# A hybrid decoder layer on one core: bonus sums from a split operand, inverse blocks moved by DMA, the pooling branch placed earlier, four staging buffers

## The chip, the cores and the metric

The kernel runs on one core of a Trainium2 chip. The metric is the time on the device in microseconds (us); lower is better. All data are fp32 in HBM. TensorE (PE) multiplies, VectorE (DVE) and ScalarE (ACT) do element work, GpSimd (POOL) does small memsets and copies, and nearly all DMAs are issued from SyncE's queue (SP).

## The reference, cut to what matters

One layer, 1024 tokens of width 1024: a projection `z = h @ w_in`, an RWKV-7 branch with 8 heads of 64, a pooling branch with windows of 2, 4, 8 and 16, an output projection with a layer norm, and then an FFN with another.

```
w_log = -softplus(-(w0 + tanh(wd) @ wl_up)) - 0.5
decay = exp(-exp(w_log))
...
# the scan over tokens, per head: state S of 64 x 64
Sa = S @ a;  S = S * w + Sa b^T + v k^T;  y = S @ r
...
var = mean(square(y - m))                    # over the 64 channels of a head
y = (y - m) * rsqrt(var + GN_EPS) * lnx_g + lnx_b
y = y + sum(r * k * r_k) * v                 # the bonus: a sum over the channels of a head
y = y * g
...
mix = concat(y_a, y_b) @ w_out;  h = LN(ALPHA * h + mix)
```

## The kernel before

The program is written in an order, and a scheduler places each instruction on its engine's queue by that order as a priority and by what is ready; the queues are then fixed. `solve` runs at high priority.

**Stages.** Input norm and projections (`z_shift`, products `pz`) come first. The scan is cut into eight tasks t = 4 s + p: s is a half of 512 tokens, p one of four groups of two heads. `fr(t)` (lines 690 to 697) makes or reloads r, k and v of a task and calls `front`. Two tasks make a pair, and `solve` (699) calls `gram`, `inverse` and `chain` for it; `chain` ends in `post`. The loop of line 707 runs `fr(t + 2)`, `fr(t + 3)` and then `solve` for pair t / 2. The pooling groups (`pool_group`, `pool_out`) stand behind that loop, at line 712; then come the weights of the output projection (`out_weights`, 727), the products `pm` of `mix` (737), and the FFN.

**front (362).** All its products with 128x512 results go through one PSUM buffer, the tag "pa" (`psa`, 194, bufs=1): pw, pq, pss, pbo and pv in turn. The decay is a polynomial of t1 = tanh(...): one ScalarE step (379), five VectorE steps (380, 381), one ScalarE step (385), and then two VectorE scans (387, 391). The bonus is `rb` (421), a product with the 0/1 matrix `bones` (423) in full fp32, which the chip runs as two passes, and a multiply by v (425). Its small tiles come from the tag "k2", six buffers.

**inverse (462).** The Gram blocks of a pair, gB, hold for each half q of the pair eight chunks of 64 x 64, and their 16 x 16 diagonal blocks are inverted by VectorE in the layout of one block per partition. To get there, `dg` (472) masks the diagonal blocks, `dc` (474) packs them by a reduction, and two DMAs (476, 477) take them through DRAM to `ab`; line 478 subtracts dg from gB. VectorE's steps of lines 488 to 512 make the inverse blocks in `ef`, once as they are and once transposed. Two DMAs per q (516, 518) bring them back as `cc`, and four multiplies with `bmask` (521) spread them over E_ and F_. Then come the products pn (535, with F_) and pzz (539, with E_).

**post (597).** ScalarE squares y, a product with `jm` (1/64 in each head's block) sums, ScalarE gives a first reciprocal root, three VectorE steps (607 to 609) refine it by one Newton step, and three more finish.

**Staging.** The weights of the output projection are loaded in 16 pieces into the tag "o" with two buffers (732, 754), and each is split by ScalarE (734) and VectorE (735) into two fp32r parts. The tiles `wo` take the place of the activations hT, which are free when the last pooling projection is done, and pool "a4" takes the place of the pooling branch's tiles (`zpool.close()`).

An fp32r operand runs in one pass; where fp32 precision is wanted, the kernel splits it in a high part (a ScalarE copy to fp32r) and a low part (a VectorE subtraction).

## Time and profile before

| what | value |
|---|---|
| median of 3 runs | 1354.23 us (1353.0 to 1354.93) |
| the profiled execution | 1357.52 us |
| its span | 1355.8 us |
| busy: PE, DVE, ACT | 1309.3, 1023.8, 526.9 us |

The span runs from the first to the last instruction of the profiled execution; the execution's own time is a little longer. A busy time is the union of an engine's instruction intervals. Matmuls overlap in a pipe, so the mean time of one is longer than their distance: what a matmul costs is read from a run of many. The idle time before an instruction is shown in brackets, with what ended it.

### The profile page before, as it was taken

Reading aid. Unit: us, or ns where it says so; the run is one execution under the profiler, and the core shown is the slowest. Engines: PE = TensorE matmul, PEld = TensorE weight load, DVE = VectorE, ACT = ScalarE, POOL = GpSimd, SP = SyncE. Lnnn points to the kernel's source line nnn. Section 1 sums busy time; section 2 is a strip of 40 time slices with the busy share of each in tenths; the row PEclk is TensorE's granted clock in tenths of the full one; section 3 lists DMA queues with packets and bytes.
Section 4 is the critical chain, followed back from the end, with each engine's and each line's share of the span. In section 5 each row is a group of like instructions: output and inputs, shape, how many; then the busy total and the mean of one; then the engine's idle time right before and its main releaser. Section 6 shows DMA issues by size and latency. Waiting matters only on the chain.

```text
span 1355.8 us, 22923 instructions
## 1 busy us (share of the span) xinstructions
PE 1309.3 (97%) x9028; PEld 1029.2 (76%) x9028; DVE 1023.8 (76%) x1807; ACT 526.9 (39%) x889; POOL 12.8 (1%) x48
## 2 busy tenths in 40 slices
PE   6999999999997989999999999999999999999997
PEld 5787777777666667778888888888888888887886
DVE  6937566569698884556889989777766767987868
ACT  5823432244334511176434333223333334553530
POOL 0000000000000000000000000000000000000000
PEclk9999999999998999999999999999999999999999
DMA  8621130122123343263433336332323237987803
GB/s 280 216 107 51 55 75 10 59 78 55 41 58 103 91 120 93 102 215 131 150 107 117 114 113 224 116 110 102 101 79 107 101 119 261 319 282 249 264 24 124
DMA packets 117101, 173.52 MB, mean 128 GB/s; under 512 B 34688, under 2 KB 43904, under 8 KB 116992
## 3 DMA queue, kind: packets, MB, share of 16 engines
q1 hardware_dynamic: 116848, 172.01, 38.8%
q8 instruction: 71, 1.16, 0.4%
q14 instruction: 38, 0.31, 0.1%
q10 hardware_dynamic: 144, 0.04, 0.0%
HBM read 124.03 MB, written 47.97 MB: 127 GB/s over the span
## 4 chain that ended last, share of the span: by engine, by line
PE 73%; DVE 14%; DMA 8%; ACT 3%; issue 2%; SPq 0%; DVEq 0%; ACTq 0%
PE p L49 31%; PE pz L49 10%; PE pgt L49 7%; PE py L49 6%; PE pm L49 5%; PE px L49 4%; DMA ar<-a_d 2%; PE pzz L49 1%; PE pg L49 1%; PE cw L49 1%; PE cs L49 1%; DMA ab<-d 1%; DMA wdr<-ff_down 1%; DVE da L830 1%; PE cu L49 1%
## 5 line engine op out<-in xcount | busy, mean ns | idle before, releaser
L49 PE MATMUL p<-tb,p 128*128 128x512 f32 x1056 | 253.0, 395 | 0.0
L49 PEld LDWEIGHTS p<-tb,p 128*128 128x128 f32 x1056 | 198.7, 188 | 47.0
L49 PE MATMUL pz<-hT,wh 128*128 128x512 f32 x576 | 190.9, 406 | 0.0
L49 PE MATMUL p<-h,p 128*128 128x512 f32 x792 | 188.6, 392 | 0.0
L49 PEld LDWEIGHTS p<-h,p 128*128 128x128 f32 x792 | 148.7, 188 | 33.0
L829 ACT CAST p<-a 128x512 fp32r<-128x512 f32 x132 | 81.2, 622 | 181.3 <-PE p L49 138.4
L49 PEld LDWEIGHTS pz<-hT,wh 128*128 128x128 f32 x576 | 107.4, 188 | 32.9 <-issue 4.7
L49 PE MATMUL pz<-hT,wl 128*128 128x512 f32 x288 | 117.5, 408 | 0.0
L830 DVE TENSOR_TENSOR p<-a,p 128x512 fp32r<-128x512 f32 x132 | 89.3, 687 | 12.5 <-ACT p L829 12.1
L49 PE MATMUL pm<-wo,mh 128*128 128x512 f32 x224 | 78.6, 418 | 3.3 <-DVE o L764 1.4
L1001 DVE TENSOR_TENSOR u<-p,u 128x512 f32<-128x512 f32 x66 | 45.3, 687 | 31.6 <-PE p L49 31.6
L49 PEld LDWEIGHTS pz<-hT,wl 128*128 128x128 f32 x288 | 54.1, 188 | 16.5 <-issue 3.8
L49 PE MATMUL px<-da 128*128 128x512 f32 x276 | 64.3, 390 | 0.0
L49 PEld LDWEIGHTS px<-da 128*128 128x128 f32 x276 | 51.8, 188 | 10.9
L49 PEld LDWEIGHTS pm<-wo,mh 128*128 128x128 f32 x224 | 41.3, 188 | 15.8 <-ACT wo L734 1.9
L245 DVE TENSOR_TENSOR wl<-wr,wh 128x512 fp32r<-128x512 f32 x36 | 24.7, 688 | 35.1 <-ACT wh L243 34.3
L49 PE MATMUL pgt<-wg,h 128*128 128x512 f32 x192 | 48.4, 396 | 0.0
L49 PE MATMUL py<-da 128*128 128x512 f32 x204 | 47.7, 389 | 0.0
L49 PE MATMUL pm<-wo,ml 128*128 128x512 f32 x112 | 46.6, 419 | 0.0
L49 PEld LDWEIGHTS py<-da 128*128 128x128 f32 x204 | 38.3, 188 | 8.1
L243 ACT CAST wh<-wr 128x512 fp32r<-128x512 f32 x36 | 22.3, 619 | 56.3 <-PE pz L49 31.8
L1022 DVE TENSOR_TENSOR gs<-p,u 128x512 f32<-128x512 f32 x44 | 30.4, 690 | 18.1 <-PE p L49 17.3
(325 smaller groups left out, 2351.0 us busy)
## 6 DMA issues: line engine op xcount, KB each, us to landing
ar<-a_d SPq DMA_DIRECT2D x77, 256.0 KB, 4.2
wdr<-ff_down SPq DMA_DIRECT2D x55, 256.0 KB, 3.8
a<-ff_gate SPq DMA_DIRECT2D x44, 256.0 KB, 2.8
a<-ff_up SPq DMA_DIRECT2D x44, 256.0 KB, 2.8
a_d<-s SPq DMA_DIRECT2D x44, 256.0 KB, 2.3
b<-ff_down SPq DMA_DIRECT2D x22, 512.0 KB, 5.8
wr<-w_in SPq DMA_DIRECT2D x36, 256.0 KB, 2.8
a_d<-gs SPq DMA_DIRECT2D x33, 256.0 KB, 2.2
```

The lines of the kernel that those rows point to most:

```text
L49: PE.matmul(o, lhsT=l, rhs=r, start=a, stop=z)
L243: S.copy(wh, wr)
L245: V.tensor_tensor(wl, wr, wh.bitcast(F32), ALU.subtract)
L829: S.copy(h, r)
L830: V.tensor_tensor(l, r, h.bitcast(F32), ALU.subtract)
L1001: V.tensor_tensor(t, ps, u, ALU.add)
L1022: V.tensor_tensor(d, ps, u, ALU.add)
```

## The change

- The bonus sums: rb is split into a high and a low fp32r part, and two products with an fp32r copy of the 0/1 matrix replace the one in fp32 (`heads`).
- The decay: the polynomial of degree six is written as a product of three squares plus constants; ScalarE makes the squares, VectorE takes two steps.
- The inverse: gB goes to DRAM as whole rows, in two DMAs per half pair (64 partitions each), into a layout in which a second view reads the diagonal blocks out. The inverse blocks are written into DRAM tiles (`d2`) that are zero elsewhere, filled once from ScalarE's queue, and read back as full E_ and F_. The masks and the packing on VectorE go; gB is multiplied by a mask of zeros on the diagonal blocks instead of the subtraction, behind the DMAs in the program.
- Post: the square is scaled ahead of the sum, so `bones` serves and `jm` goes; the Newton step takes one square on ScalarE and two steps on VectorE; a factor of -0.5 goes into the column `hlg`.
- The pooling groups stand ahead of `fr(6)` and `fr(7)` in the program's order.
- The tag "o" has four buffers.

The lists QB, QE and QS hold the constants of the three squares; that hunk is left out.

```diff
@@ -65,10 +67,10 @@
     V.memset(bones[64:128, 64:128], 1.0)
-    jm = cq.tile([128, 128], F32, name="jm")
-    V.tensor_scalar(jm, bones, 1.0 / 64, None, ALU.mult)
+    bonr = cq.tile([128, 128], F32R, name="bonr")
+    V.tensor_copy(bonr, bones)
     cmat = cq.tile([128, 128], F32, name="cmat")
-    V.tensor_tensor(cmat, ident, jm, ALU.subtract)
+    V.scalar_tensor_tensor(cmat, bones, -1.0 / 64, ident, ALU.mult, ALU.add)
     gmask = cq.tile([128, 128], F32, name="gmask")
@@ -83,6 +85,9 @@
                         compare_op=ALU.is_ge, fill=0.0, base=15, channel_multiplier=-1)
+    omask = cq.tile([128, 64], F32, name="omask")
+    V.tensor_scalar(omask.rearrange("p (q t) -> p q t", q=4), bmask[:, :, None].to_broadcast([128, 4, 16]),
+                    -1.0, 1.0, ALU.mult, ALU.add)
     e0 = cq.tile([128, 65 * NC + 1], F32, name="e0")
@@ -93,9 +98,9 @@
     V.memset(epsg, GN_EPS)
-    qb = cq.tile([128, 2], F32, name="qb")
-    V.memset(qb[:, 0:1], DECAY[5])
-    V.memset(qb[:, 1:2], DECAY[0])
+    qb = cq.tile([128, 4], F32, name="qb")
+    for i, c in enumerate(QB + [QE[1]]):
+        V.memset(qb[:, i:i + 1], c)
@@ -110,6 +115,8 @@
     V.tensor_scalar(oka, col[:, KA:KA + 4], -0.5, 1.0, ALU.mult, ALU.add)
+    hlg = cq.tile([128, 4], F32, name="hlg")
+    V.tensor_scalar(hlg, col[:, LG:LG + 4], -0.5, None, ALU.mult)
     lor = cq.tile([128, 512], F32, name="lor")
@@ -198,6 +205,15 @@
+        def heads(ps, t, tile):
+            h, l = tile("sh", F32R), tile("sl", F32R)
+            S.copy(h, t)
+            V.tensor_tensor(l, t, h.bitcast(F32), ALU.subtract)
+            mm(ps, bonr, h, True, False)
+            mm(ps, bonr, l, False, True)
@@ -376,13 +392,17 @@
             pc = k2("pc")
-            S.activation(pc, t1, AF.Identity, scale=DECAY[6], bias=qb[:, 0:1])
-            for n in (0.0, DECAY[4], DECAY[3], DECAY[2], DECAY[1]):
-                V.scalar_tensor_tensor(pc, pc, n, t1, ALU.add, ALU.mult)
+            pd = k2("pd")
+            S.activation(pc, t1, AF.Square, bias=qb[:, 0:1])
+            S.activation(pd, t1, AF.Square, bias=qb[:, 1:2])
+            S.activation(pd, pd, AF.Identity, bias=qb[:, 3:4])
+            S.activation(t1, t1, AF.Square, bias=qb[:, 2:3])
+            V.scalar_tensor_tensor(pc, pc, QE[0], pd, ALU.add, ALU.mult)
+            V.scalar_tensor_tensor(pc, t1, QE[2], pc, ALU.add, ALU.mult)
             wx = k2("wx", w=65 * NC + 1)
...
             wx3 = wx[:, 0:65 * NC].rearrange("p (c t) -> p c t", t=65)
-            S.activation(wx3[:, :, 1:65], v3(pc), AF.Identity, bias=qb[:, 1:2])
+            S.activation(wx3[:, :, 1:65], v3(pc), AF.Copy, scale=QS)
             Ep = s2.tile([128, NC, 65], F32, name="Ep", tag="ep", bufs=1)
@@ -420,7 +440,7 @@
             pb = psa("pbo")
-            mm(pb, bones, rb, True, True)
+            heads(pb, rb, k2)
             bv = s2.tile([128, 512], F32, name="bv", tag="bv", bufs=4)
@@ -459,6 +479,23 @@
+        HS = 64 * 64 + 64
+        def rows_of(d, h):
+            return d.rearrange("(c h r) -> c h r", c=NC, h=2)[:, h, 0:64 * 64].rearrange("c (p t) -> p c t", t=64)
+        def blocks_of(d):
+            return d.rearrange("(g r) -> g r", g=64)[:, 0:1024].rearrange("g (s t) -> g s t", t=64)[:, :, 0:16]
+        d2 = [[dp.tile([2 * NC * HS], F32, name=f"d2{q}{x}", bufs=1) for x in range(2)] for q in range(2)]
+        zt = s1.tile([128, 2 * NC * HS // 128], F32, name="zt", tag="k2", bufs=KA_BUFS)
+        G.memset(zt, 0.0)
+        for q in range(2):
+            for x in range(2):
+                nc.scalar.dma_start(d2[q][x].rearrange("(p r) -> p r", p=128), zt)
@@ -466,16 +503,10 @@
             for q in range(2):
-                A4 = gB[:, q, :, 0:64].rearrange("p c (q t) -> p c q t", q=4)
-                dg = kb("dg")
-                dg4 = dg.rearrange("p c (q t) -> p c q t", q=4)
-                V.tensor_tensor(dg4, A4, bmask[:, None, :, None].to_broadcast([128, NC, 4, 16]), ALU.mult)
-                dc = s1.tile([128, NC, 16], F32, name="dc", tag="dc", bufs=2)
-                V.tensor_reduce(dc, dg.rearrange("p c (q t) -> p c t q", q=4), AX.X, ALU.add)
-                d1 = dp.tile([NC, 128, 16], F32, name="d1", tag="d1", bufs=4)
-                nc.sync.dma_start(d1.rearrange("c p t -> p c t"), dc)
-                nc.sync.dma_start(abf[QR[q], 0:256], d1.rearrange("c (a s) t -> (c a) (s t)", a=8))
-                V.tensor_tensor(gB[:, q, :, 0:64], gB[:, q, :, 0:64], dg, ALU.subtract)
+                d1 = dp.tile([2 * NC * HS], F32, name="d1", tag="d1", bufs=4)
+                for h, R in enumerate(HR):
+                    nc.sync.dma_start(rows_of(d1, h), gB[R, q, :, 0:64])
+                nc.sync.dma_start(abf[QR[q], 0:256].rearrange("g (s t) -> g s t", t=16), blocks_of(d1))
             eff = s1.tile([128, 528], F32, name="ef", tag="ef", bufs=1)
@@ -512,16 +543,17 @@
             for q in range(2):
-                d2 = dp.tile([2 * NC, 128, 16], F32, name="d2", tag="d2", bufs=4)
-                nc.sync.dma_start(d2.rearrange("(x c) (a i) t -> (c a) x (i t)", x=2, i=16), ef[QR[q]])
-                cc = s1.tile([128, 2 * NC, 16], F32, name="cc", tag="cc", bufs=2)
-                nc.sync.dma_start(cc, d2.rearrange("g p t -> p g t"))
                 E_, F_ = [s1.tile([128, NC, 64], F32, name=n, tag=n, bufs=2) for n in ("ex", "fx")]
-                for i, t in ((1, F_), (0, E_)):
-                    V.tensor_tensor(t.rearrange("p g (q t) -> p g q t", q=4),
-                                    cc[:, NC * i:NC * i + NC, None, :].to_broadcast([128, NC, 4, 16]),
-                                    bmask[:, None, :, None].to_broadcast([128, NC, 4, 16]), ALU.mult)
                 EF.append((E_, F_))
+            for i in (1, 0):
+                for q in range(2):
+                    nc.sync.dma_start(blocks_of(d2[q][i]), ef[QR[q], i, :].rearrange("g (i t) -> g i t", t=16))
+                for q in range(2):
+                    for h, R in enumerate(HR):
+                        nc.sync.dma_start(EF[q][i][R], rows_of(d2[q][i], h))
+            for q in range(2):
+                V.tensor_tensor(gB[:, q, :, 0:64], gB[:, q, :, 0:64],
+                                omask[:, None, :].to_broadcast([128, NC, 64]), ALU.mult)
@@ -599,16 +631,16 @@
             ys = pt("ys")
-            S.activation(ys, py, AF.Square)
+            S.activation(ys, py, AF.Square, scale=0.125)
             pvv = chp.tile([128, 512], F32, name="pvv", tag="ch")
-            mm(pvv, jm, ys, True, True)
+            mm(pvv, bones, ys, True, True)
             y0 = pt("y0")
             S.activation(y0, pvv, AF.Abs_reciprocal_sqrt, bias=epsg)
-            V.scalar_tensor_tensor(ys, pvv, GN_EPS, y0, ALU.add, ALU.mult)
-            V.scalar_tensor_tensor(ys, ys, -0.5, y0, ALU.mult, ALU.mult)
-            V.scalar_tensor_tensor(y0, ys, 1.5, y0, ALU.add, ALU.mult)
+            S.activation(ys, y0, AF.Square)
+            V.scalar_tensor_tensor(ys, pvv, GN_EPS, ys, ALU.add, ALU.mult)
+            V.scalar_tensor_tensor(y0, ys, 3.0, y0, ALU.subtract, ALU.mult)
             V.tensor_tensor(ys, py, y0, ALU.mult)
-            V.scalar_tensor_tensor(ys, ys, col[:, LG + p:LG + p + 1], d["bv"], ALU.mult, ALU.add)
+            V.scalar_tensor_tensor(ys, ys, hlg[:, p:p + 1], d["bv"], ALU.mult, ALU.add)
             pg = chp.tile([128, 512], F32, name="pgate", tag="ch")
@@ -704,21 +736,24 @@
         fr(1)
+        pools = []
         for t in range(0, 8, 2):
+            for g in ({4: (3, 2, 1, 0)}).get(t, ()):
+                pools.append(pool_group(g))
+                if len(pools) > 1:
+                    pool_out(g + 1, *pools[-2])
+                if g == 0:
+                    pool_out(0, *pools[-1])
             if t < 6:
...
             solve(tk[t // 2])
-        pools = [pool_group(3)]
-        for g in (2, 1, 0):
-            pools.append(pool_group(g))
-            pool_out(g + 1, *pools[-2])
-        pool_out(0, *pools[-1])
         zpool.close()
...
         s4 = ostk.enter_context(tc.tile_pool(name="a4", bufs=2, side="right"))
+        OB = 4
         wo = act_tiles("wo")
@@ -729,7 +764,7 @@
                     h, l = wo_part(i, cf)
-                    r = s4.tile([128, 512], F32, name="wr4", tag="o", bufs=2)
+                    r = s4.tile([128, 512], F32, name="wr4", tag="o", bufs=OB)
                     nc.sync.dma_start(r, w_out[128 * k:128 * k + 128, 512 * cf:512 * cf + 512])
@@ -751,7 +786,7 @@
                 if tt < 4:
-                    o = s4.tile([128, 512], F32, name="o", tag="o", bufs=2)
+                    o = s4.tile([128, 512], F32, name="o", tag="o", bufs=OB)
                     nc.sync.dma_start(o, h_d[tsl, cs])
...
                     o = acc[tt][:, cs]
```

## Rows read from the trace of the kernel before

**Rows 1.** The page's part 1: busy us (share of the span) xinstructions.

```profile
PE 1309.3 (97%) x9028; PEld 1029.2 (76%) x9028; DVE 1023.8 (76%) x1807; ACT 526.9 (39%) x889; POOL 12.8 (1%) x48
```

**Rows 2.** Engine times by stretch; columns in the first line.

```profile
core 0: us, PE busy (x) PEld busy (x) DVE busy (x) ACT busy (x) POOL busy (x), PEclk, DMA share, GB/s
100.00:171.00 71.00, 70.78 (x367) 52.76 (x367) 45.41 (x73) 29.07 (x47) 2.23 (x3) 1.00 0.17 54
171.00:302.00 131.00, 128.63 (x1386) 96.90 (x1386) 83.84 (x165) 43.13 (x76) 2.02 (x8) 0.97 0.19 56
302.00:388.00 86.00, 80.52 (x1198) 59.45 (x1196) 72.39 (x150) 34.84 (x61) 3.41 (x10) 0.98 0.20 52
388.00:478.00 90.00, 81.25 (x1179) 58.17 (x1178) 78.18 (x158) 41.69 (x72) 2.15 (x8) 0.94 0.32 86
478.00:560.00 82.00, 77.50 (x1109) 58.09 (x1105) 50.00 (x111) 14.68 (x32) 0.00 (x0) 1.00 0.32 91
```

**Rows 3.** Timeline of fronts 4 and 5: start, us, engine, line, what [idle before].

```profile
312.58 1.12 PE L49 MATMUL pw<-lw,lor 64*128 64x512 f32 x2
...
344.42 0.74 DVE L421 SCALAR_TENSOR_TENSOR rb<-r,col,kp 128x512 f32<-128x512 f32 x1
345.85 1.12 PE L49 MATMUL pbo<-rb,bones 128*128 128x512 f32 x2
...
354.82 1.12 PE L49 MATMUL pw<-lw,lor 64*128 64x512 f32 x2
```

**Rows 4.** Timeline of the inverse in the solve after 302 us.

```profile
303.83 1.29 DVE L449 TENSOR_TENSOR gB<-pg,gmask 128x512 f32<-128x512 f32 x2
...
307.52 1.03 DVE L474 TENSOR_REDUCE dc<-dg 128x128 f32<-128x512 f32 x1
308.58 0.37 SPq L476 DMA_DIRECT2D d<-dc  x1
311.23 0.48 SPq L477 DMA_DIRECT2D ab<-d  x1
313.46 0.17 DVE L490 TENSOR_TENSOR tm<-ef,ab 128x4 f32<-128x4 f32 x1 [0.47 <-DMA ab<-d]
...
321.07 1.29 SPq L516 DMA_DIRECT2D d<-ef  x2
323.51 1.41 SPq L518 DMA_DIRECT2D cc<-d  x2
326.45 0.69 DVE L521 TENSOR_TENSOR fx<-cc,bmask 128x512 f32<-128x512 f32 x1
327.20 3.22 PE L49 MATMUL pn<-fx,gB 64*64 64x64 f32 x64 [1.99 <-DVE fx L521]
330.21 2.56 PE L49 MATMUL pzz<-ex,fx 64*64 64x64 f32 x64
```

**Rows 5.** Pieces of the chain that ended last: start, us, what.

```profile
61.62 42.19 PE pz L49 x180
...
478.24 1.05 PE pbo L49 x2
```

**Rows 6.** Groups by line: out<-in shapes xcount, busy us, mean ns, idle.

```profile
L381 DVE SCALAR_TENSOR_TENSOR pc<-pc,t 128x512 f32<-128x512 f32 x40 | 27.4, 686 | 10.8 <-ACT pc L379 10.3
L474 DVE TENSOR_REDUCE dc<-dg 128x128 f32<-128x512 f32 x8 | 8.2, 1029 | 0.0
L379 ACT ACTIVATE pc<-t,qb 128x512 f32<-128x512 f32 x8 | 5.7, 710 | 0.0
```

**Rows 7.** The DRAM tiles d (d1 and d2): issue to landing of their DMAs.

```profile
DMA to landing us min/median/max: 2.0/2.4/4.0
```

**Rows 8.** Stretch after 410 us: SyncE's queue, and engine times as in rows 2.

```profile
410.00:420.00 10.00, 5.49 (x48) 3.18 (x50) 9.88 (x17) 2.33 (x4) 1.49 (x3) 0.66 0.69 159
...
419.56 0.81 SPq L733 DMA_DIRECT2D wr<-w_out  x2
...
434.25 1.18 SPq L733 DMA_DIRECT2D wr<-w_out  x2
```

More of the change, by code (lines that the diff above doesn't have):

```diff
@@ L29 @@
 GN_EPS = 1e-5 * 64
-DECAY = [7.38403150e-01, -2.23932079e-01, 3.39554149e-02, -3.43247040e-03,
-         2.60245296e-04, -1.58445669e-05, 7.95516283e-07]
+QB = [2.6446236909266547, -4.777402204072105, -7.825890616949517]
+QE = [148.19110777287312, 64.07475031771858, 7.586255131509925]
+QS = 7.95516283e-07
 MU, W0, A0, KK, KA, RK, LG, LB, PS, IG, IB, MG, MB = 0, 14, 18, 22, 26, 30, 34, 38, 42, 46, 54, 62, 70
```

## The prediction

> **What bounds the kernel now.** I read the page's busy times first, then a table of engine times by stage, then the order of events inside one stage, and the forms of single instructions last. By busy time TensorE is nearly full, 97% of the span, with VectorE at 76% and ScalarE at 39% [rows 1]. The stage table shows that the three do not stand alike everywhere. Up to 302 us the projections keep TensorE full: 70.78 of 71 us, then 128.63 of 131. In the three stages after it, each with one solve (gram, inverse, chain, post) and, in the first two, two fronts, TensorE is idle for 5.5, 8.8 and 4.5 us, 18.7 us together, while VectorE is busy for 72.39 of 86, 78.18 of 90 and 50.00 of 82 us [rows 2]. Everything behind 602 us (output of the mix, FFN) is not touched by the change and is TensorE's alone; it carries through unchanged.
>
> What orders the stages from 302 us on is a ring of one PSUM buffer. The tag "pa" has one buffer, through which pw, pq, pss, pbo and pv of a front go one after the other, so front 5 can't start its pw before front 4's pv has been copied. From one pw (312.58) to the next (354.82) is 42.2 us, and 31.8 of them lie between pw and rb, the operand of the bonus matmul: work of VectorE, which has the solve's and the pools' work in between [rows 3]. The other chain is the inverse of the pair: from the last masked Gram block to the first product pn, 305.1 to 327.2, with four DMA landings in it; TensorE stood still for 1.99 us ahead of pn [rows 4].
>
> **The change part by part.** *Bonus sums.* One fp32 product with two passes took 1.05 us; 180 products with fp32r operands of the same size took 42.19 us, 0.234 each [rows 5]. Two of those are 0.47 us, so 0.58 us less per front and 8 x 0.58 = 4.7 us of TensorE in all. The price is a ScalarE copy (0.71 us at most by the ACT row) and a VectorE subtract (0.69) between rb and the matmul, on the ring: 1.4 - 0.6 = 0.8 us later for pv and the next pw [rows 3, 6]. Fronts 0 to 3 run where TensorE is full: 4 x 0.58 = 2.3 us count there in full.
>
> *Decay.* Five VectorE steps at 0.686 us become two, one ScalarE step ahead of them becomes four at up to 0.71, the step behind them stays one [rows 6]. In time from t1 to wx that is 5 x 0.69 + 2 x 0.71 = 4.9 us against 2 x 0.69 + 5 x 0.71 = 4.9: the path alone gains nothing; what is gained is VectorE's time, 3 x 0.69 per front. With the new subtract a front is 2 x 0.69 = 1.4 us of VectorE cheaper, a pair 2.7. The three new k2 tiles per front (16 allocations through six buffers instead of 13) cost nothing as long as the ring of one PSUM buffer is what holds the next front back; bounds 0 to the 0.8 us above.
>
> *Inverse.* Per half (q), VectorE loses a multiply (0.69) and a reduction (1.03) ahead of the DMA and two multiplies (2 x 0.69) behind it; the subtract on gB becomes a multiply of the same size, and it moves behind the DMAs [rows 4, 6]. Per pair 2 x (1.72 + 1.37) = 6.2 us. The first half of the path gets shorter: now the last gB is done at 303.83 + 1.29 = 305.1, dg and dc end at 308.6, the write has landed at 311.2, the read at 313.46. Changed, the two half writes can be issued at 305.1 and 305.5 (0.37 us each on SyncE's queue), land after 2.0 to 4.0 us, and the read takes about as long as now, 2.2, with more and shorter pieces: 309.7 to 311.7, say 310.2, so 3 us earlier, 1.7 at the bad end [rows 4, 7]. The second half: F goes through a write (2.44 us from issue to the next issue) and reads (2.94 now), then straight into pn. F's first half lands at about 321.07 + 0.65 + 2.44 + 0.4 + 2.5 = 327.1 or, if its reads are quicker than the 128 KB read of now, up to a microsecond earlier: pn starts about where it does now, 327.2, -1 to +1.4. E is issued behind F, four writes and reads later: by the same sum 329.7 to 332.4, where pzz, its first user, starts now at 330.21 [rows 4]. I take F at 0 and E at +1, so a solve is 2 us shorter, with 0.4 longer and 4 shorter as ends.
>
> Eighteen DMAs replace eight per pair on SyncE's queue, ten more at 0.37 to 0.65 us of issue, 3.7 to 6.5 us of that queue per solve. The new waits (each group of reads for its write) stand in SyncE's order; behind them are the loads of rkv for the next front, the stores of ya, and the loads of w_out. The rkv loads run a front ahead, so a wait of some 2.5 us is covered by the 42 us of the ring; uncovered it would be paid once per solve. The four zero fills are on ScalarE's queue behind a POOL memset, at the end of the input stage, with ScalarE at 29.07 of 71 us afterwards [rows 2]: cost 0, bounds 0 to 3 us once, covered by the full TensorE of that stage.
>
> Here a rule of the Trainium skill speaks against the change: "DMA: Bandwidth & Descriptors", section "Rules for kernel authors", says that two transfers to disjoint halves of the partitions serialize and that one transfer over 128 should be used instead. This trace has no pair of such halves of one tile to show it. By that rule the half write would land at about 305.1 + 2 x 2.4 = 309.9 and the first part of the path would gain 1 us or less instead of 3; a solve would then be as long as now, and my sum below would be some 3 us smaller.
>
> *Post.* Six VectorE steps become five, one more Square on ScalarE; 2 x 0.69 = 1.4 us of VectorE per pair, the path unchanged. The new constants are small single operations at the start, where VectorE waits for loads: 0.
>
> *ScalarE's price.* Per pair 2 x (3 + 1) + 2 = 10 more operations at 0.71, 7.1 us, on 34.84 busy of 86 us [rows 2, 6]: it stays under half.
>
> *Pooling and staging.* The pools were already filler beside fronts 4 and 5; ahead of front 6 in the order only the last group moves. What changes is when the old activations and the pool's buffers come free. Now the loads of w_out begin at 419.56 with two, and the next two begin only at 434.25, since each of the two staging buffers is held until VectorE has split it. In the 10 us ahead of that TensorE works 5.49, and with those gaps its granted clock has a mean of 0.66, between the levels 1.2 and 2.4 GHz [rows 8]. With four buffers twice as many loads are out before VectorE is needed, so the output products that fill TensorE's gaps are ready sooner. The work is the same; I count it inside the idle time below, 0 to 5 us.
>
> **The sum.** A pair costs VectorE 2.7 + 6.2 + 1.4 = 10.3 us less, out of 72 and 78 busy in the two stages with fronts. Three pairs lie in the stages from 302 us on: 31 us. Not all of it reaches the end, since TensorE is busy for over 90% there and its work does not shrink but for the bonus. The visible idle time of 18.7 us is what a shorter ring and a shorter inverse can take away at first hand; I take 15 of it, that is half of VectorE's 31, since the chain of small products keeps some waits whatever VectorE does. With the 2.3 us of fronts 0 to 3, and 1.2 for the bonus of half of the other fronts, the sum is -18.5 us. The profiled execution took 1357.5 us for a span of 1355.8, so 1339.0; it lies 3.3 us above the median of the runs, 1354.2, so I predict 1335.7, rounded to 1336. Ends of this case: only a quarter of the 31 us and the full TensorE share, 1354.2 - 7.7 - 3.5 = 1343; all of the 31, the bonus in full and 2 us ahead of pn in the first solve: 1354.2 - 31 - 4.7 - 2 = 1316.
>
> **The rivals.** *TensorE is the bound after all.* If the static order leaves as many gaps, and only the cheaper bonus product shows, 1354.2 - 4.7 = 1349.5. For it: 97% busy. Against it: the idle times of the stages and the clock under full speed in the 410 us row.
> *The ring pays back what VectorE gives.* The copy and the subtract lengthen it by 0.8 us, four ScalarE steps in a row may wait behind the chain's scalings, about 2 us per front; four fronts after 302 us make 4 x (0.8 + 2 - 1.4 x 2) = 0 and the bonus 2.3 us: 1352, no change that can be told. For it: ring and ScalarE's order are strict. Against it: VectorE is fuller than ScalarE.
> *E comes too late (slower).* If SyncE's queue keeps the order of the program, E's writes go out only after F's reads, and E's reads after those, two rounds of 2.44 + 2.94 us plus issue: E at 321.1 + 13 = 334 or later, 4 us or more behind now, and 2 us more for the loads held behind. pzz waits in each of four solves, 4 x 6 = 24 us, against some 16 us of gain that remain elsewhere: 1354.2 + 24 - 16 = 1362. It decides from about 4 us per solve. For it: pzz stood right behind pn, with nothing between. Against it: now both writes are issued ahead of both reads (321.07 x2, 323.51 x2), not in the order of the program [rows 4], so the order is made by readiness.
> *The change doesn't do what it says.* Staging and pools may leave the times of the w_out loads as they are, since the space is the pools' until they end; that takes at most 5 us from the forecast and is in its range.
>
> **How the numbers follow.** Forecast 0.60 at 1336 (1316 to 1345), TensorE-bound 0.14 at 1349.5, ring 0.10 at 1352, late E 0.16 at 1362. A measurement of this kernel can tell about 0.2%, 2.7 us. Faster than 1351.5: 0.74; within: 0.10; slower than 1356.9: 0.16. The range 1316 to 1356 leaves out the late E and a small tail below.
>
> **What would show it.** Right: pw to pw in the stages from 302 us near 37 us instead of 42; last gB to the first tm 5 to 6 us instead of 8.4; no wait ahead of pn over 1 us; VectorE about 41 us less busy over the span; w_out's loads four at a time. Wrong: waits of pzz for a DMA of E; the ring as long as before; TensorE's idle time from 302 to 560 us still near 19 us, which would mean that the order of the instructions and not VectorE's time sets the stages.

## The result, and the profile after

The changed kernel takes 1367.24 us (median of 4 runs, 1365.56 to 1367.77) against 1354.58 for the kernel before beside it (4 runs): a ratio of 1.0085, with a 95% interval from 1.0067 to 1.0104. It is 13 us slower; the forecast was 1336, and the nearest of the rivals "E comes too late" at 1362. Its profiled execution has a span of 1363.8 us, 8.0 more than the one before; at the first product p of the FFN it is 11.3 (717.14 against 705.86 us). The page's part 1 of the kernel after (busy us, share of the span, instructions):

```profile
PE 1315.6 (96%) x9028; PEld 1025.7 (75%) x9028; DVE 989.6 (73%) x1755; ACT 550.8 (40%) x929; POOL 15.0 (1%) x49
```

Its engine times in the stretches of [rows 2], with the same columns:

```profile
100.00:171.00 71.00, 67.66 (x351) 50.18 (x351) 37.46 (x61) 31.98 (x52) 2.23 (x3) 1.00 0.18 53
171.00:302.00 131.00, 128.42 (x1389) 94.83 (x1388) 76.76 (x155) 50.55 (x89) 2.91 (x8) 1.00 0.25 64
302.00:388.00 86.00, 82.29 (x1183) 60.63 (x1184) 64.72 (x141) 38.64 (x69) 4.62 (x13) 0.98 0.28 67
388.00:478.00 90.00, 78.60 (x1051) 52.59 (x1053) 69.55 (x138) 47.46 (x83) 1.74 (x5) 0.89 0.46 125
478.00:560.00 82.00, 81.85 (x1110) 61.24 (x1105) 43.62 (x98) 14.43 (x30) 0.00 (x0) 1.00 0.33 83
```

VectorE did get lighter: 989.6 us against 1023.8 [rows 1], 34 less. But TensorE has new gaps in two places: 67.66 of 71 us in the first stretch, where it was full, and 78.60 of 90 in the fourth, at a granted clock of 0.89 instead of 0.94 [rows 2]. Over the five stretches it is as busy as before, 438.8 us against 438.7, but with some 155 matmuls fewer: they are left for later. The solve shows what is late. The timeline of the kernel after for the solve that [rows 4] shows of before, cut to its two transfers and to some of TensorE's products behind the second:

```profile
305.25 0.69 DVE L469 TENSOR_TENSOR gB<-pg,gmask 128x512 f32<-128x512 f32 x1 [0.27 <-PE pg L51]
305.97 1.27 SPq L508 DMA_DIRECT2D d<-gB  x2
310.94 1.21 SPq L257 DMA_DIRECT2D wr<-w_in  x2
312.27 1.03 SPq L509 DMA_DIRECT2D ab<-d  x1
316.62 0.17 DVE L521 TENSOR_TENSOR tm<-ef,ab 128x4 f32<-128x4 f32 x1 [3.66 <-DMA ab<-d]
...
324.40 2.75 SPq L550 DMA_DIRECT2D d<-ef  x4
327.25 0.62 SPq L553 DMA_DIRECT2D ex<-d  x1
327.97 2.62 SPq L553 DMA_DIRECT2D fx<-d  x4
330.64 1.98 SPq L553 DMA_DIRECT2D ex<-d  x3
332.70 0.33 PE L51 MATMUL pn<-fx,gB 64*64 64x64 f32 x2
...
334.55 1.14 PE L51 MATMUL pn<-fx,gB 64*64 64x64 f32 x30
335.62 0.50 PE L51 MATMUL pz<-hT,wl 128*128 128x512 f32 x1
...
336.51 0.32 PE L51 MATMUL pn<-fx,gB 64*64 64x64 f32 x2
...
338.01 0.63 PE L51 MATMUL pz<-hT,wh 128*128 128x512 f32 x2
...
338.81 1.14 PE L51 MATMUL pn<-fx,gB 64*64 64x64 f32 x30
...
340.78 1.14 PE L51 MATMUL pzz<-ex,fx 64*64 64x64 f32 x30
```

The second transfer is twelve DMAs, issued one behind another on SyncE's queue from 324.40 to 332.6: four writes in 2.75 us, then eight reads, one about every 0.65 us. The main groups of pn stand at 334.55 and 338.81, 10 and 14 us behind the first write; before, both halves of pn ran at 327.20, 6 us behind it [rows 4]. In this solve the first transfer is longer as well: the read of ab waits behind two loads of w_in (310.94) and lands at 316.6.

The issue of the DMAs is the smaller part of this delay. The four reads of F landed 3.5 to 3.7 us after their issue in this solve, so F was whole at 333.6; of the 32 products of its second half two ran at 336.51 and the other thirty from 338.81 on, since products pz stood ahead of them in TensorE's fixed order. No product pn had a wait ahead of it in the kernel after. The same, over the four solves, for this kernel and some of those of the experiments below, in us from the first write of ef (F and E are whole when the last read has landed, or the last multiply with bmask has ended):

```
                          before  after    e2     f2     f3     f4     g3
F whole                      8.3    9.6    9.5    8.8   14.5   11.0   10.4
E whole                      8.9   11.7   11.7   11.0   15.1   11.0   11.7
last product pn starts      10.0   16.0   14.3   14.2   16.6   19.6   13.9
last addition rr ends       19.5   27.0   26.1   26.0   25.2   28.6   23.0
other products between F
and the last pn, a solve       0     11      9      9      3     20      2
```

F and E are whole 1.3 and 2.7 us later than before, the last pn starts 6.0 later and the last addition ends 7.5 later. Some 5 of the 7 us lie between operand and product, where the scheduler's order has other products. Why it has them there with these transfers is not shown: no run changed TensorE's order alone.

Over the four solves I measured two legs: from the last masked Gram block to the first tm, and from the copy of ef to the last addition rr. The first went from 8.5 us on average (7.3, 8.3, 9.3, 9.2) to 7.9 (6.6, 10.7, 8.2, 6.0), the second from 19.6 (22.3, 17.1, 19.8, 19.0) to 26.6 (26.9, 25.6, 29.1, 24.7). A solve is 6.4 us longer, and the solves stand in series, as VectorE's rows on gB between the second and the third solve show (the last of the chain's copies, then the first block of the next pair; kernel after, then kernel before):

```profile
385.98 0.29 DVE L609 COPY gB<-cu 128x128 f32<-128x128 f32 x1 [0.55 <-PE cu L51]
387.95 0.68 DVE L469 TENSOR_TENSOR gB<-pg,gmask 128x512 f32<-128x512 f32 x1
```

```profile
369.47 0.27 DVE L577 COPY gB<-cu 128x128 f32<-128x128 f32 x1
371.48 0.68 DVE L449 TENSOR_TENSOR gB<-pg,gmask 128x512 f32<-128x512 f32 x1
```

In both kernels the next Gram block is written 2.0 us after the last copy of the chain: gB has one buffer (the tile is allocated with bufs=1), and the chain uses it to its end. That it is this buffer that holds the next block is read from the program and the distance; gK and kt have one buffer too, and no run gave any of them a second. What a solve's path gains or loses is carried into the next solve; the last copy of the last chain stands at 570.23 us instead of 550.03. TensorE fills such time with other products as long as there are any; behind 388 us there are not enough (a table for 388 to 440 us stands under f3).

### The profile page after: what moved, and what is told of

It reads as the page before. It is cut to its first block, busy times and chain, and to the rows that moved or that the text cites. A ratio compares the mean times of both kernels' runs of the same rounds, so it can differ in the third digit from the quotient of the medians.

```text
span 1363.8 us, 22970 instructions
## 1 busy us (share of the span) xinstructions
PE 1315.6 (96%) x9028; PEld 1025.7 (75%) x9028; DVE 989.6 (73%) x1755; ACT 550.8 (40%) x929; POOL 15.0 (1%) x49
## 4 chain that ended last, share of the span: by engine, by line
PE 86%; DVE 6%; DMA 3%; ACT 3%; issue 1%; SPq 0%; DVEq 0%; ACTq 0%
PE p L51 31%; PE pz L51 11%; PE py L51 8%; PE px L51 8%; PE pm L51 7%; PE pgt L51 7%; PE pg L51 2%; PE pzz L51 1%; PE cw L51 1%; PE cs L51 1%; PE cu L51 1%; PE pn L51 1%; PE pk L51 1%; DMA acc<-m_d 1%; PE pt L176 1%
## 5 line engine op out<-in xcount | busy, mean ns | idle before, releaser
L51 PE MATMUL pz<-hT,wh 128*128 128x512 f32 x576 | 194.7, 410 | 1.3 <-ACT zc L293 1.0
L51 PE MATMUL pm<-wo,mh 128*128 128x512 f32 x224 | 84.5, 441 | 3.7 <-issue 3.7
L261 DVE TENSOR_TENSOR wl<-wr,wh 128x512 fp32r<-128x512 f32 x36 | 24.7, 688 | 36.9 <-ACT wh L259 36.9
L51 PEld LDWEIGHTS pg<-ga,bk 64*64 64x64 f32 x512 | 28.8, 138 | 18.6 <-DVE gB L469 4.3
```

The costliest lines, as they stand in the source:

```text
L51: PE.matmul(o, lhsT=l, rhs=r, start=a, stop=z)
L261: V.tensor_tensor(wl, wr, wh.bitcast(F32), ALU.subtract)
```

## The experiments

All times are medians; the kernel before stood beside each group of runs, at 1353.1 (e), 1353.6 (f), 1353.3 (g), 1353.5 (h) and 1352.3 us (i). The theories of the first four, by the names in their expectations: T1, the issue of eighteen DMAs lengthens each solve; T2, the pools ahead of the last front use up TensorE's other work; T3, ScalarE's longer order holds the fronts.

### Which part of the change: e1 to e4

Each takes parts of the change over as the diff has them (in e1, e4, g4 and h1 two small constants share one tile, for space).

```
e1: bonus, squares, post, pools ahead     (inverse and two staging buffers as before)
e2: the inverse by DMA alone
e3: all but the pools ahead
e4: bonus, squares, post
```

> The changed kernel with the inverse's blocks moved as in the kernel before (masks and packing on VectorE, eight DMAs per pair) and two staging buffers, since four don't fit in the room that this inverse leaves; the columns hka and oka share a tile for 32 bytes of room. Theory 1 (the eighteen DMAs per pair, issued one after the other at about 0.65 us each, make every solve longer): faster than before, 1335 to 1345. Theory 2 (the pooling groups ahead of front 6 use up TensorE's filler and hold front 6 back, 410 against 399 us, and the inverse is innocent): still slower, 1360 or more. Theory 3 (ScalarE's longer order in the fronts): 1355 to 1362.

Measured: 1354.6, ratio 1.0004 (0.9991 to 1.0018).

> The kernel before with the inverse by DMA alone. Theory 1: slower than before, 1370 to 1380, with E landing some 11 us after the copy of ef. Theory 2 and theory 3: 1348 to 1356, since VectorE has 6 us less per pair and nothing else moves.

Measured: 1366.4, ratio 1.0086 (1.0071 to 1.0101).

> The changed kernel with the pooling groups behind the loop again. Theory 1: 1362 to 1370, hardly other than the changed kernel. Theory 2: 1340 to 1350, TensorE's stretch without work after 410 us gone. Theory 3: 1362 to 1367.

Measured: 1369.7, ratio 1.0119 (1.0097 to 1.0141).

> The kernel before with the split bonus operand, the three squares and the new post alone. Theory 1 and theory 2: faster, 1338 to 1348, by TensorE's 4.7 us and VectorE's 4.1 us per pair. Theory 3: 1355 or more.

Measured: 1351.3, ratio 0.9981 (0.9967 to 0.9996).

The inverse by DMA alone carries the loss (e2), although it takes 21 us of VectorE's time away (page part 1: DVE 1002.6). T2 falls: without the pools ahead (e3) the change is no faster. T1 has the side of the loss, though less of it than its 1370 to 1380, and the gain it promised for the rest did not come: e1 gives nothing and e4 2 us.

### Which transfer, and what a hop costs: f1 to f4

f1 takes the first transfer alone, f2 the second alone:

```diff
 f1, first transfer
-    V.tensor_tensor(dg4, A4, bmask[...], ALU.mult)
-    V.tensor_reduce(dc, dg..., AX.X, ALU.add)
-    nc.sync.dma_start(d1..., dc)
...
+    for h, R in enumerate(HR):
+        nc.sync.dma_start(rows_of(d1, h), gB[R, q, :, 0:64])
+    nc.sync.dma_start(abf[QR[q], 0:256]..., blocks_of(d1))
...
```

> Before, with the first transfer of the inverse alone taken from the change (the whole Gram rows go to DRAM, the diagonal blocks come back, a multiply by omask takes the place of the subtract); the second transfer (cc, bmask, VectorE) is as before. Theory S (the solve is the serial path: the next pair's Gram can't begin before this pair's chain has left the one buffer of gB, so a microsecond of it costs about half a microsecond of the whole, 13 us for 4 x 6.5): the first leg, last gB to the first tm, is 0 to 1.5 us shorter per solve, so 1350 to 1353. Rival V (VectorE's time sets the end): 3.4 us less VectorE per pair would be worth 5 us or more, 1345 to 1349. Rival Q (SyncE's longer queue costs by itself): 1355 to 1359.

Measured: 1344.95, ratio 0.9942 (0.9920 to 0.9963): the first transfer gains 8.7 us and beats both kernels. That is the fast end of rival V's range, and more than theory S allowed.

> Before, with the second transfer of the inverse alone taken from the change (blocks written into zero-filled DRAM, E and F read back as whole tiles); the first transfer is as before. Theory S: the second leg, end of the ef copy to the last rr, is 6 to 8 us longer in every solve, which carries nearly the whole loss: 1363 to 1368. Rival Q (it is the number of DMAs on SyncE's queue, in both legs): about half of the loss, 1357 to 1361. Rival V: 2.7 us less VectorE per pair, 1348 to 1352.

Measured: 1367.15, ratio 1.0104 (1.0081 to 1.0127): the whole loss, as theory S had it. Its second leg is 26.1, 26.9, 24.2, 24.7 us. Rival V falls with it as a rule for the whole: VectorE is 9 us less busy over the span (1014.8) and the kernel 13.5 slower. The first leg of f1 is 7.4, 7.4, 7.1, 8.7 us, 0.9 shorter on average; its timeline in the second solve:

```profile
299.66 1.29 DVE L452 TENSOR_TENSOR gB<-pg,gmask 128x512 f32<-128x512 f32 x2
300.98 1.26 SPq L482 DMA_DIRECT2D d<-gB  x2
...
305.11 1.01 SPq L483 DMA_DIRECT2D ab<-d  x1
...
308.32 0.17 DVE L495 TENSOR_TENSOR tm<-ef,ab 128x4 f32<-128x4 f32 x1 [2.47 <-DMA ab<-d]
```

The 3.5 us of VectorE from the last block to the issue for dc are gone, but write and read take 4.1 and 3.2 us instead of 2.65 and 2.2 [rows 4]; of the 4.1, 1.0 is the read's, which had to wait behind a load of w_in on SyncE's queue after the second write had landed at 304.10.

> Before, with one DMA more from DRAM to DRAM between the write of d2 and the read of cc, in each half of a pair: two small DMAs more per solve on the path, VectorE's work unchanged. It measures what a microsecond of the solve's path costs. Theory S: the second leg is 2.5 to 4 us longer in each of four solves, at half a microsecond each 5 to 8 us in all, 1358 to 1361. Rival V, or TensorE alone as the bound: the path is covered, 1352 to 1355.

```diff
     nc.sync.dma_start(d2..., ef[QR[q]])
+    nc.sync.dma_start(dh, d2)          # DRAM to DRAM, both halves
-    nc.sync.dma_start(cc, d2...)
+    nc.sync.dma_start(cc, dh...)
```

Measured: 1363.8, ratio 1.0082 (1.0055 to 1.0108), with a second leg of 25.2 us on average, 5.6 more: 10.2 us for 22.6 us of path. So the path is paid, at about half, with VectorE's work unchanged; path and time are both more than theory S had (2.5 to 4 us, 1358 to 1361). Where TensorE pays is seen in the stretch from 388 to 440 us of four kernels (columns as in [rows 2]; before, after, f2, f3):

```profile
388.00:440.00 52.00, 44.89 (x749) 33.70 (x749) 45.99 (x96) 20.91 (x35) 1.96 (x7) 0.90 0.32 82
```

```profile
388.00:440.00 52.00, 40.81 (x410) 24.99 (x410) 38.21 (x73) 26.32 (x43) 1.43 (x3) 0.80 0.56 143
```

```profile
388.00:440.00 52.00, 36.19 (x448) 21.94 (x448) 41.89 (x80) 23.03 (x34) 1.21 (x4) 0.84 0.35 92
```

```profile
388.00:440.00 52.00, 35.38 (x400) 21.82 (x399) 43.30 (x83) 23.55 (x37) 1.23 (x4) 0.80 0.36 97
```

TensorE is busy 4 to 10 us less there, and its mean clock falls from 0.90 to 0.80 to 0.84, so some of what it does runs at the lower of its two levels.

> Before with the whole inverse by DMA, but E and F of a half pair lie side by side in one tile and come back with one read per partition half: four reads instead of eight in a solve, the same bytes and the same pieces. Theory S with serial issue (0.65 us per read on SyncE's queue): the last read goes out some 2.6 us earlier, the second leg is 23 to 25 us instead of 26 to 27, and the total 1360 to 1364. Rival P (the pieces of 256 bytes and their landing of 3.3 us and more set it, not the count of DMAs): 1364 to 1368.

```diff
-    E_, F_ = [s1.tile([128, NC, 64], ...) for n in ("ex", "fx")]
+    X = s1.tile([128, 2, NC, 64], ...)          # E and F side by side
+    for h, R in enumerate(HR):
+        nc.sync.dma_start(X[R]..., both halves of d2 in one read)
```

Measured: 1367.95, ratio 1.0110 (1.0085 to 1.0134). Four reads for eight gained nothing: a read of 256 KB lands 4.7 us after its issue (median) where one of 128 KB took 3.1 in f2, and pn, which needs F alone, now waits for E's bytes too (second leg 30.0, 28.0, 27.8, 26.2). With half the reads E is whole as late as in f2, 11.0 us behind the first write, F 2.1 later, and TensorE's order puts 20 other products between F and the last pn. The count of issues does not set the leg.

### Where a delay is paid, and two queues: g1 to g4

g1 and g2 put f3's hop into the first two or the last two solves.

> Before, with the one hop more from DRAM to DRAM in the second transfer of the first two solves only; the last two are as before. With the hop in all four the total was 1363.8, 10 us over before. Theory S (the four solves are one serial path, a delay counts wherever it falls): half of it, 1357 to 1360, and the lost time of TensorE shows up late, behind 390 us, where filler has run out. Rival W (only a delay inside the third solve, where TensorE has least other work, is paid): 1352 to 1355.

Measured: 1355.7, ratio 1.0022 (1.0011 to 1.0033).

> Before, with the hop in the last two solves only; the first two are as before. Theory S: half, 1357 to 1360. Rival W: nearly all of it, 1361 to 1365.

Measured: 1359.7, ratio 1.0061 (1.0037 to 1.0085). Neither theory has it right: +2.4 and +6.3, together 8.7 of f3's 10.2. A late delay costs more. In g1 the third and the fourth solve make up for some of it (the last copy of the last chain at 553.77, 3.7 later than before; in g2 562.23, in f3 567.60).

> Before with the whole inverse by DMA (1366.4 as one queue), but the second half pair's writes and reads of E and F are issued by ScalarE's queue instead of SyncE's; the same transfers and bytes. Theory I (serial issue on one queue, 0.65 us per DMA, sets the 7 us of the second leg): six of twelve issues leave the queue, the leg ends 3 to 4 us earlier, 1358 to 1362. Rival P (each transfer's own time from issue to landing, 3.3 us and more for pieces of 256 bytes, sets it): 1364 to 1368. ScalarE's own order may hold its half back, which would be worse than either: 1369 or more.

```diff
-    nc.sync.dma_start(...)                      # both halves q
+    for q, dma in enumerate((nc.sync.dma_start, nc.scalar.dma_start)):
+        dma(blocks_of(d2[q][i]), ef[QR[q], i, :]...)
+        dma(EF[q][i][R], rows_of(d2[q][i], h))
```

Measured: 1350.2, ratio 0.9986 (0.9971 to 1.0001), 16 us less than the same transfers on one queue (e2). The second leg is 22.5 us on average instead of 25.4. Each transfer takes longer, not shorter (median to landing 4.1 us for fx on ScalarE's queue, 3.1 in e2), and F and E are whole no earlier, 10.4 and 11.7 us behind the first write against 9.5 and 11.7 in e2. So it is not the issue that is saved. The gain lies on TensorE: two other products and not nine between F and the last pn, and 9.0 us and not 11.8 from there to the last addition. TensorE waits for reads of F here, 12.6 us in all, and never does in e2; the solve is shorter even so. The time lies below the ranges of both theories; the trace is of an execution of 1356.2 us, 6 above the median.

> Before with the first transfer by DMA (1345.0 alone), the bonus sums in two parts, the squares on ScalarE and the shorter post (1351.3 alone); the second transfer, the pools and the staging are as before. If the two gains add up: 1341 to 1344. If the longer path of the front (copy and subtract ahead of the bonus product, TensorE waiting for bk at 123.8 us in both kernels with these edits) takes its own gain back once the solve is shorter: 1345 to 1350.

Measured: 1349.6, ratio 0.9973 (0.9963 to 0.9983). The gains don't add up; the math edits take 4.7 us back.

### Which of the math edits, and the change on two queues: h1 to h4

h1, h2 and h3 are f1 with the bonus, the squares or the post, each as in the diff; h4 is the whole change with g3's two queues.

> Before with the first transfer by DMA (1345.0) and the bonus sums in two parts, nothing else. Theory A (the copy and the subtract ahead of the bonus product lengthen the ring through the one buffer of pa, and TensorE waits in the first fronts): 1347 to 1350. Rival (the cheaper product shows, 4.7 us less TensorE, and the math's loss lies in the squares): 1340 to 1343.

Measured: 1346.0 (0.9956, 0.9941 to 0.9970). Nothing that can be told from f1, either way.

> Before with the first transfer by DMA (1345.0) and the decay by squares on ScalarE, nothing else. Theory A: 1344 to 1346, since the path from t1 to wx is as long by either form. Rival B (four ScalarE steps in a row wait behind the chain's scalings, and every front gets later): 1347 to 1351.

Measured: 1351.2 (0.9979, 0.9967 to 0.9990): the squares cost 6.3 us.

> Before with the first transfer by DMA (1345.0) and the shorter post, nothing else: one VectorE step less at the end of each half pair, off the solve's path. Theories A and B both: 1343 to 1346. Over 1347 would mean that the post's added ScalarE step holds the next front.

Measured: 1345.2 (0.9939, 0.9925 to 0.9953). Nothing either way.

> The whole change, with the second half pair's writes and reads of E and F on ScalarE's queue instead of SyncE's. Theory I (twelve issues on one queue are the change's loss): 16 us less than the changed kernel's 1367.2, as for the inverse alone, so 1349 to 1353. Rival O (another part of the change costs as much): 1358 or more.

Measured: 1369.7 (1.0115, 1.0102 to 1.0128). Two queues do not cure the whole change, although the second leg is 3.1 us shorter than in the kernel after (23.4) and the last copy of the last chain 6 us earlier. What the squares do is seen in ScalarE's copies of the projections out of PSUM (r<-pz), in the timelines of f1 and then of h2:

```profile
114.98 0.69 ACT L276 ACTIVATE r<-pz,omu 128x512 f32<-128x512 f32 x1 [2.38 <-PE pz L49]
119.92 0.69 ACT L276 ACTIVATE r<-pz,omu 128x512 f32<-128x512 f32 x1
```

```profile
120.40 1.24 ACT L278 ACTIVATE r<-pz,omu 128x512 f32<-128x512 f32 x2
```

The stretch around them, f1 and then h2, columns as in [rows 2]:

```profile
100.00:171.00 71.00, 70.78 (x366) 53.16 (x365) 43.53 (x70) 29.06 (x47) 2.22 (x3) 1.00 0.19 57
```

```profile
100.00:171.00 71.00, 68.28 (x349) 50.71 (x348) 35.76 (x57) 31.77 (x52) 2.22 (x3) 0.98 0.17 53
```

With the squares the first copy comes 5.4 us later, behind the front's chain, and from there work is put off: VectorE does 7.8 us less in this stretch and TensorE, full in f1, loses 2.5. The kernel after has the same mark, 67.66. In h4 the squares meet the second queue. ScalarE's rows in the second solve, and the scan of VectorE that waits for it:

```profile
325.60 1.34 ACTq L550 DMA_DIRECT2D d<-ef  x2
326.99 0.72 ACT L398 ACTIVATE pd<-pd,qb 128x512 f32<-128x512 f32 x1 [3.14 <-issue]
...
331.39 1.28 ACTq L552 DMA_DIRECT2D fx<-d  x2
332.71 0.73 ACTq L552 DMA_DIRECT2D ex<-d  x1
338.20 0.58 ACT L566 COPY fx<-pn 128x512 f32<-128x512 f32 x1 [9.30 <-PE pn L51]
338.68 0.63 ACT L405 ACTIVATE wx<-pc 128x512 f32<-128x512 f32 x1
```

```profile
339.42 1.24 DVE L407 TENSOR_TENSOR_SCAN Ep<-wx,e 128x520 f32<-128x520 f32 x1 [10.19 <-ACT wx L405]
```

The step wx of the front stands in ScalarE's order behind the reads and behind the copy of pn, and the scan waits 10.19 us for it (3.87 in g3, where wx stands behind the same copy).

### Without the squares, and fewer DMAs in the first transfer: i1 and i2

> The whole change without the squares (the decay stays five VectorE steps), with the second half pair's writes and reads of E and F on ScalarE's queue. Theory B+I (with the squares four ScalarE steps of a front stand behind DMA issues that wait for transfers; without them ScalarE has little to hold): 1347 to 1353. Rival O (pools ahead of the last front or the staging cost the 16 us): 1360 or more.

Measured: 1361.3 (1.0060, 1.0043 to 1.0078). Without the squares h4 gains 8.4 us, but 11 over g3 remain. They lie in the bonus, the post, the pools ahead and the staging taken together; the first two cost nothing on top of f1, where ScalarE issues no reads. Which of them it is was not tried, nor whether ScalarE's copy for the bonus costs more behind the reads on its queue.

> Before with the first transfer by DMA (1345.0 with six DMAs per pair: four writes of half a tile, two reads), now with three: one write for each partition half over both half pairs, and one read over all 128 partitions. The same bytes and pieces. Theory I (issues one behind another at 0.37 to 0.65 us): last gB to the first tm 6 to 6.5 us instead of 7.6, and 1341 to 1344. Rival P (a transfer twice as large lands later by what the issues save; the first half pair's write also can't go out ahead of the second's Gram): 1345 to 1349.

```diff
-    for q in range(2): two writes of d1, one read of ab
+    for h, R in enumerate(HR):
+        nc.sync.dma_start(d1 rows of both q, gB[R, :, :, 0:64]...)
+    nc.sync.dma_start(abf[:, 0:256]..., blocks of both q)
```

Measured: 1358.8 (1.0046, 1.0031 to 1.0060), 14 us slower than f1. SyncE's queue in the second solve:

```profile
300.30 1.30 SPq L481 DMA_DIRECT2D d<-gB  x2
...
306.86 0.39 SPq L484 DMA_DIRECT2D ab<-d  x1
...
309.95 0.17 DVE L498 TENSOR_TENSOR tm<-ef,ab 128x4 f32<-128x4 f32 x1 [0.61 <-DMA ab<-d]
```

The read now goes out 6.6 us behind the writes instead of 4.1, since writes of 256 KB land after 4.1 us (median) and not 2.5 (here the second at 304.84), and since it stands behind a load of rkv on SyncE's queue in this solve. The first half pair's blocks no longer travel while the second's Gram is made. The first leg is 11.5 us on average. Rival P, and by more than it said: against the six DMAs of f1, three are the worse.

## Why the prediction was wrong

*The second transfer.* This is the step that failed first. I took F at 0 (bounds -1 to +1.4) and E at +1, and let pn and pzz follow at once, as one write, one read and a multiply had them follow before. The landings are at the bad ends of that or just past them: counted from the first write, the first pn starts 8.6 us behind it on average (7.2 before), and E is whole at 11.7, where I had 8.6 to 11.3. What I had at nothing is the rest: the second half of F, and TensorE's order. The last pn starts 6.0 us later than before, 6.4 behind its landed operand instead of 1.6, and the second leg is 7 us longer. The issue of the DMAs (3.7 to 6.5 us per solve) I had put on "SyncE's queue" as cover for loads; it is in the 1.3 and 2.7 us by which F and E are late.

The rival "E comes too late" had the side, and its 1362 is nearest by luck. No pzz waits for a read of E, all four writes go out ahead of the reads (324.40 x4), and without the 16 us of gain elsewhere, which did not exist, its own sum gives 1378.

*The ring.* I had the order of the stages go by the PSUM buffer pa. That ring did get shorter, as forecast: pw to pw 35.4 us (314.67 to 350.07) against 42.2 [rows 3]. It bought nothing, because the solves stand in series, by the program through the one buffer of gB, and that chain got longer. Two more of my signs of being right came with the slower kernel, no wait ahead of pn over 1 us and four loads of w_out at a time: they show that engines are free, not that the path is short. Over all twenty kernels measured here, the start of the last chain's last copy and the time go together (correlation 0.95, 0.9 us of time per us, by a straight line through the twenty points; the copy is read from one execution, the time is the median, and with that execution's own time it is 0.93 and 0.8):

```
kernel   last copy   time        kernel   last copy   time
h1         544.6    1346.0       e1         559.7    1354.6
f1         545.0    1345.0       g2         562.2    1359.7
h3         545.8    1345.2       i1         564.1    1361.3
h2         548.0    1351.2       h4         564.3    1369.7
before     550.0    1353.5       e2         566.7    1366.4
g4         553.3    1349.6       f3         567.6    1363.8
g1         553.8    1355.7       f2         568.5    1367.2
e4         554.2    1351.3       f4         569.7    1368.0
g3         555.7    1350.2       after      570.2    1367.2
i2         559.1    1358.8       e3         573.5    1369.7
```

It is a relation, with up to 7 us beside the line (h4), and not a price: f3 paid 0.45 us per us of second leg, and g1 and g2 show that the place matters.

*VectorE's half.* "Half of VectorE's 31 us reaches the end" is the term that made the forecast fast, and the whole change gives it no support: 34 us less VectorE (41 forecast) came with 13 us more, 16 us less in e4 with 2. Only f1, 12 us less with 8.7, would fit it.

*The first transfer.* Forecast 3 us earlier per solve, 1.7 at the bad end; measured 0.9 in f1. The term that was mis-sized is "the read takes about as long as now, 2.2" and the time from the write's issue to the read's: 3.2 and 4.1 us. The Trainium skill, "DMA: Bandwidth & Descriptors", section "Rules for kernel authors", says that two transfers to disjoint halves of the partitions serialize, from which I had worked out a gain of 1 us or less. The size fits, the reason isn't seen: the half writes of the kernel after land 2.6, 2.7 and 3.2 us after their issue (shortest, median, longest), and not the second at twice the first. The trace of the kernel before did have such a pair, which I overlooked: the two writes of ef [rows 4], issued 0.68 us apart in that solve, landed 2.4 us after their issue, each of them. These 0.9 us came with a gain of 8.7 in f1, where the second leg was shorter by 1.6 as well (18.0), so each solve by 2.5. At f3's price that is 4.5 us of the 8.7; where the other 4 come from is not shown.

*The bonus product.* 8 x 0.58 = 4.7 us of TensorE was mis-sized. The groups of pbo of the kernel after, then of before (count, busy us, mean ns):

```profile
L51 PE MATMUL pbo<-sh,bonr 128*128 128x512 f32 x8 | 3.9, 487 | 0.0
L51 PE MATMUL pbo<-sl,bonr 128*128 128x512 f32 x8 | 3.5, 433 | 0.0
```

```profile
L49 PE MATMUL pbo<-rb,bones 128*128 128x512 f32 x16 | 8.9, 638 | 0.8 <-DVE rb L421 0.7
```

7.4 us against 8.9, so 1.5 in all: 0.234 each is the pace inside a row of 180, not the time of two alone.

*The squares.* "The path alone gains nothing" was right and not enough. I had ScalarE's price at none since it stays under half busy; the rival of the ring had four ScalarE steps that may wait. On top of f1 they cost 6.3 us, and the trace has copies out of PSUM that come later.

*Pools and staging.* Forecast 0 to 5 us of gain. The loads of w_out do go out four at a time, from 407.31, in place of two at 419.56 [rows 8]; but the pools ahead cost 3.3 us over e4 (e1) and come with 2.5 less beside the DMA inverse (after against e3, two groups of runs); neither is far from the noise. Four buffers by themselves were not tried.

## What to carry to other kernels

Before costing an engine's time, find what is serial: a tile with one buffer, used from the first step of a stage to its last, makes a chain, and a microsecond counts by where it lies on that chain, not by the engine that it frees. Replacing element work by DMA paid where it took steps off that chain (f1) and lost where its operands came in many pieces (f2). Do not stop at the landing of an operand: look in the trace for when its user starts, and what the user's engine has ahead of it in its order. Here that was 5 of 7 us: fewer DMAs did not take it away (f4), and a kernel whose operands landed no earlier lost much of it (g3). Work moved to an engine with idle time still takes a place in that engine's order, ahead of what others wait for.

## What the runs showed of the hardware

- A read or write of 64 partitions took 0.57 to 0.82 us of issue on SyncE's queue in the second transfer of the kernel after (medians 0.61 to 0.67), and several follow each other at that pace: 2.75 us for four.
- Transfers of 128 KB in pieces of 256 bytes landed 2.5 to 2.7 us after their issue as writes (medians of f1 and the kernel after) and 3.1 to 3.8 as reads from SyncE's queue (e2, f2, the kernel after); of 256 KB, after 4.1 (writes, i2) and 4.7 (reads, f4). More bytes for one issue was no gain here.
- Issuing half of them from ScalarE's queue came with 16 us less (g3 against e2), though each transfer then landed later and the last of E no earlier (11.7 us behind the first write in both). The Trainium skill, "DMA: Bandwidth & Descriptors", section "Issuing engines are not separate DMA queues", says that this saves only the time of issue, "usually small relative to the DMA itself". The landings agree; what the kernel gained lies behind them, in TensorE's order.
- What stands behind a DMA's issue on ScalarE waits with it: 3.14 us ahead of pd in h4, behind two writes of ef.
